# Two edits in one: expert low parts on VectorE alone with pinned one-hot rows, and bytes left unused ahead of pools so that both operands of a matmul begin at the same offset modulo 512

## The chip, the cores and the metric

The kernel runs on one core of a Trainium2 chip. A core has TensorE (PE), VectorE (DVE), ScalarE (ACT), GpSimd (POOL) and the sync engine (SP), which issues most of the DMAs. The metric is the device time of the whole program in microseconds.

## What is computed

A diffusion-style block of two layers is followed by a second block with a mixture of experts. There are 1024 tokens of width 1024. Cut to what matters here:

```python
def even_mixer(hx, ...): qa, ..., gb = split_cols(h @ w_in, ...)      # layer 0: attention, then w_out
def gla_mixer(hx, ...):  q, k, v, g, ... = h @ w_in                    # layer 1: gated linear attention, then w_out

def mixer_layer(u, ...):                                               # second block, 1040 rows (16 are meta tokens)
    a, bv, bg, q, k, v, fg, gates = split(u @ w_in)
    ya = pool_mixer(a, ...) @ w_out_a
    yb = conv_module(bv, bg, ...) @ w_out_b
    yc = forgetting_attention(heads(q), heads(k), heads(v), logf) @ w_out_c
    return (g[:, :, 0] * ya + g[:, :, 1] * yb + g[:, :, 2] * yc) @ w_o

def hier_moe(t, ...):                                                  # 16 experts, the top 2 of one group for each token
    for e in range(N_EXPERTS):
        he = silu(t @ exp_w1[e]) * (t @ exp_w3[e])
        y = y + comb[:, e:e + 1] * (he @ exp_w2[e])

return rms_norm_2(h[:, N_META:], final_g)
```

All products are of float32 inputs.

## The kernel before

**Products in three parts.** A float32 operand is split in two fp32r tiles: the high part `h` is a cast by ScalarE (L161), the low part `l` is the operand less its high part, a subtraction (L164). `split_into` does both; its last argument puts the subtraction on VectorE ("v") or GpSimd ("p"). `mm3` then adds three products in PSUM: L168, L169 and L170 are high by high, low by high and high by low. In the trace `pj<-sloth,u2h` reads: into `pj`, moving operand `sloth` (a weight slot's high part, 512 columns wide), stationary operand `u2h` (128 rows wide).

**Stages**, in order, by the time of the profile: projections of layer 0 from `h0`, up to 490 us; its attention, to 850; the Bridge (`omT` times w_out) and layer 1's projections from `h1`, to 1310; the scans of layer 1, to 1465; the second Bridge, to 1545; the projections of the mixer from `u2`, to 2091; fox (the forgetting attention), to 2240; the merge (products `my` of `yabT` and `ycT`), to 2365; w_o (again `omT`) with the router, to 2485; the experts, to 2758; the tail with the last adds and the final norm, to 2793.5.

**Experts.** Tokens are gathered into 24 tiles of 128: experts 0 to 6 have two tiles, the others one, and the two kinds alternate; a 17th group takes what overflows. For each tile, `turned` transposes the gathered rows `xg` into `xT`, `hidden` computes `ph` (24 products by `w13`) and `he`, `hidden_turned` transposes `he` to `hT`, and `result` computes `y` (12 products by `w2`), which is added to `acc` in DRAM by an indirect DMA. An expert's weights come as six raw pieces of 512 KB (four `w13`, two `w2`) through 13 buffers, and each is split into its two parts. A counter sends every third low part to GpSimd. GpSimd also issues the gathers and the scatters.

**Tail.** The last two tiles' `y` is not scattered but split once more (`xTl<-y`), and added to the eight row blocks of `acc` by products with one-hot matrices (L2255): 16 tiles of 128x128, made by VectorE at L2229 in `slots_by_token`. The adds are L2256. `scaled` does the final norm of a row block: a `Square` on ScalarE into a buffer named `y`, `rr`, and a multiplication (L2244).

**What sets the order.** A scheduler orders each engine's queue when the program is built, by its own estimates; a tile that shares bytes with an older one in another pool can be written only after the older one's last use. The rest is by semaphores as the data arrives.

Of the kernel before, what the change touches and what calls it, by code (L numbers as in the profile page):

```python
# [27 lines left out]
ORD = (0, 1, 2, 3, 8, 9, 4, 5, 6, 7)  # L28
WB = 8
# [39 lines left out]
class Ctx:  # L69
    pass  # L70

# [374 lines left out]
def layer0(k, x, ctxt):  # L446
# [188 lines left out]
    with ExitStack() as es:  # L635
        kvp = es2.enter_context(tc.tile_pool(name="kv", bufs=1))
        V = kvp.tile([128, NTC, 640], F32, name="V")
# [188 lines left out]
class Bridge:  # L826
# [26 lines left out]
    def pools(self, es, res, dst, hT, off, a_col, b_col):  # L853
        self.__dict__.update(locals())
        tc = self.k.tc
        self.px = es.enter_context(tc.tile_pool(name=f"px{self.layer}", bufs=1))
        self.es2 = ExitStack()
        self.p = self.es2.enter_context(tc.tile_pool(name=f"op{self.layer}", bufs=1))

    def gate(self, c):  # L860
        g = self.p.tile([128, D], F32, name="gate")
        self.k.nc.scalar.dma_start(g, bc_rows(self.k.dgate[self.layer, c], D))
        return g

    def turn(self, i, bank=None, place=None):
        k, nc = self.k, self.k.nc
        if place:
            mt = self.row
        else:
            mt = self.p.tile([128, D], F32, name="om")  # L870
            nc.sync.dma_start(mt, self.dm[i])
        m = []
        for b in range(2):
            pt = bank() if bank else self.ps.tile([128, 4, 128], F32, name="tp", bufs=3)
            for j in range(4):
                nc.tensor.transpose(pt[:, j, :], mt[:, (4 * b + j) * 128:(4 * b + j + 1) * 128], k.ident)
            if place:
                o, t = Ctx(), place(b)
                o.h, o.l = t[:, 0], t[:, 1]
            else:  # L880
                o = Split(self.p, [128, 4, 128], "omT", 3)
            split_into(k, pt, o.h, o.l)
            m.append(o)
        return m
# [327 lines left out]
T2 = S + NM  # L1212
LAGF = 3
# [23 lines left out]
def mixer2(k, br, x1, x2):  # L1237
# [20 lines left out]
    with es:  # L1258
        hp = es.enter_context(tc.tile_pool(name="u2", bufs=1))
        uT = Split(hp, [128, 8, T2], "u2")  # L1260
        g1 = k.vec["norm1"]
        es3 = ExitStack()
        br.pools(es3, lambda i: x1[i], lambda i: x2[i], uT, NM, g1[:, None, :], None)
# [18 lines left out]
        tslices = [(0, 348), (348, 346), (694, 346)]  # L1282
# [256 lines left out]
    yp = es0.enter_context(tc.tile_pool(name="ycT", bufs=1))  # L1539
    ycT = Split(yp, [128, 4, S], "ycT")  # L1540
    NB = NT + 1
    with ExitStack() as es:
        kvp = es.enter_context(tc.tile_pool(name="fkv", bufs=1))

        p2, p = (es.enter_context(tc.tile_pool(name=n, bufs=1)) for n in ("fw2", "fw"))
        wo = k.wo = Ctx()
# [193 lines left out]
def moe(k, dm, x2, out):  # L1740
# [53 lines left out]
    with ExitStack() as es:  # L1794
# [189 lines left out]
        def row(name):  # L1984
            return mp.tile([128, 16], F32, name="R" + name)
# [59 lines left out]
        pc2 = mp.tile([128, 1], F32, name="pc2")  # L2045
# [24 lines left out]
    def tiles(raw_tile, groups, keep=0, hooks=None, ahead=1, pre=()):  # L2070
# [5 lines left out]
        def expert_split(raws):  # L2076
            w13 = Split(p, [128, 8, 512], "w13", 1 + ahead)
            w2 = Split(p, [128, 2, 1024], "w2", 2)
            yield w13, w2
            for q in range(2):  # L2080
                for a in range(2):
                    k.ndma += 1
                    c = (slice(None), slice(4 * q, 4 * q + 4), slice(256 * a, 256 * a + 256))
                    split_into(k, next(raws), w13.h[c], w13.l[c], "a", "v" if k.ndma % 3 else "p")
                    yield
            for q in range(2):
                k.ndma += 1
                split_into(k, next(raws), w2.h[:, q, :], w2.l[:, q, :], "a", "v" if k.ndma % 3 else "p")
                yield
# [10 lines left out]
        def turned(t, x):  # L2100
# [5 lines left out]
            xT = Split(p, [128, 8, 128], "xT", 2)  # L2106
            for b in range(2):
                pt = ps.tile([128, 4, 128], F32, name="xt", bufs=4)
                for j in range(4):
                    nc.tensor.transpose(pt[:, j, :], x[:, (4 * b + j) * 128:(4 * b + j + 1) * 128], k.ident)  # L2110
                split_into(k, pt, xT.h[:, 4 * b:4 * b + 4], xT.l[:, 4 * b:4 * b + 4])
            return xT, w
# [107 lines left out]
    def slots_by_token():  # L2220

        fg.append(raw_tile([128, D]))
        nc.scalar.dma_start(fg[0], bc_rows(A["final_g_2"], D))
        for t in last_tiles:
            sm = mp.tile([128, NT], F32, name="sm", bufs=KEEP)
            nc.vector.tensor_scalar(sm, th, -1.0, sl[:, t:t + 1], op0=OP.mult, op1=OP.add)
            P = raw_tile([128, NT, 128], F32R)
            for i in range(NT):
                nc.vector.tensor_scalar(P[:, i, :], cnt, sm[:, i:i + 1], None, op0=OP.is_equal)  # L2229
            to.append(P)  # L2230

    def rows():

        for i in range(NT):
            X.append(raw_tile([128, D]))
            nc.sync.dma_start(X[i], acc[i * 128:(i + 1) * 128, :])

    def scaled(p, i):
# [3 lines left out]
        nc.scalar.activation(p.tile([128, D], F32, name="y", bufs=2), x, AF.Square, accum_out=ss)  # L2242
# [4 lines left out]
    es, p, ps, kept = tiles(raw_tile, groups, KEEP, {-KEEP - 1: slots_by_token, -KEEP: rows}, pre=[chain(pre, rest)])  # L2247
    for i in range(NT):
# [8 lines left out]
        scaled(p, i)  # L2257
# [3 lines left out]
    with tc.If(nx > NXS):  # L2261
        with tc.tile_pool(name="exraw2", bufs=1) as rp2:
# [6 lines left out]
            for i in range(NT):  # L2269
                nc.sync.dma_start(X[i], acc[i * 128:(i + 1) * 128, :])  # L2270
                scaled(rp2, i)
# [43 lines left out]
```

## Time and profile before

| | |
|---|---|
| time, median of 3 runs | 2800.44 us (2799.43 to 2801.71) |
| profiled execution | 2795.24 us, span 2793.5 us |
| granted TensorE clock, mean | 0.979 |
| TensorE busy | 2645.3 us, 95% of the span, 15970 matmuls |
| VectorE, ScalarE, GpSimd busy | 55%, 38%, 21% |
| DMA | 405.33 MB, 145 GB/s on average |

A matmul's duration is modelled and overlaps the next; where TensorE doesn't stand still, the time between two starts is what a matmul costs. Idle time is read from the waits: an engine, the line it waited in, and what released it.

### The profile page before, as it was taken

How to read it: one execution, taken by the hardware profiler on the slowest of the kernel's cores; microseconds unless marked ns; L12 is line 12 of the kernel's file. 1: busy time of each engine (PE TensorE's matmuls, PEld its weight loads, DVE VectorE, ACT ScalarE, POOL GpSimd, SP SyncE). 2: the span in 40 equal slices, each digit the busy share in tenths (PEclk: the TensorE clock that was granted, in tenths of full speed). 3: DMA queues.
4: the chain of work that ended last, by engine and by line, in shares of the span. 5: the costliest groups of instructions: out<-in, count | busy, mean ns of one | idle time of the engine just before them, and what ended most of it. 6: DMA issues, size and time to landing. Idle time of an engine off the chain costs nothing. (4 is left out here: it accounts for less than half of the span.)

```text
span 2793.5 us, 41767 instructions
## 1 busy us (share of the span) xinstructions
PE 2645.3 (95%) x15970; PEld 2172.5 (78%) x15970; DVE 1536.0 (55%) x2972; ACT 1066.6 (38%) x2035; POOL 580.9 (21%) x515
## 2 busy tenths in 40 slices
PE   8999999999999999999999999999999999969995
PEld 3777778887887778887887887788878977857774
DVE  5467747887886461100884434373206655357886
ACT  4333321666663332112642332222316621246563
POOL 1334400012211110012541120000000033025662
PEclk9999999999999999999999999999999999979998
DMA  7233387546224353222654123232437157449995
GB/s 249 83 90 106 114 214 213 183 92 121 66 51 164 108 184 106 86 76 101 200 193 151 60 84 106 91 117 83 125 122 174 32 165 253 143 171 325 312 317 173
DMA packets 273570, 405.33 MB, mean 145 GB/s; under 512 B 28338, under 2 KB 156585, under 8 KB 272721
## 3 DMA queue, kind: packets, MB, share of 16 engines
q1 hardware_dynamic: 255360, 365.79, 42.7%
q0 software_dynamic: 6624, 24.14, 3.4%
q10 hardware_dynamic: 11376, 12.64, 1.4%
q8 instruction: 128, 2.10, 0.3%
q14 instruction: 82, 0.66, 0.1%
HBM read 290.35 MB, written 112.15 MB: 144 GB/s over the span
## 5 line engine op out<-in xcount | busy, mean ns | idle before, releaser
L164 DVE TENSOR_TENSOR slotl<-slotraw,sloth 128x1024 fp32r<-128x1024 f32 (+2 forms) x100 | 116.8, 1170 | 282.7 <-ACT sloth L161 226.6
L168 PE MATMUL pj<-sloth,u2h 128*128 128x512 f32 (+1 forms) x592 | 237.4, 401 | 0.0
L169 PE MATMUL pj<-slotl,u2h 128*128 128x512 f32 (+1 forms) x592 | 234.8, 397 | 0.0
L170 PE MATMUL pj<-sloth,u2l 128*128 128x512 f32 (+1 forms) x592 | 233.2, 394 | 0.0
L168 PE MATMUL pj<-wh,h0h 128*128 128x512 f32 (+1 forms) x560 | 216.2, 386 | 0.3 <-DVE h0h L338 0.3
L169 PE MATMUL pj<-wl,h0h 128*128 128x512 f32 (+1 forms) x560 | 212.3, 379 | 0.5 <-DVE wl L164 0.4
L170 PE MATMUL pj<-wh,h0l 128*128 128x512 f32 (+1 forms) x560 | 211.4, 378 | 0.0
L169 PE MATMUL pj<-slotl,h1h 128*128 128x512 f32 x432 | 168.7, 391 | 0.0
L168 PE MATMUL pj<-sloth,h1h 128*128 128x512 f32 x432 | 168.7, 390 | 0.0
L170 PE MATMUL pj<-sloth,h1l 128*128 128x512 f32 x432 | 168.5, 390 | 0.0
L161 ACT CAST sloth<-slotraw 128x1024 fp32r<-128x1024 f32 (+2 forms) x100 | 99.6, 999 | 152.8 <-PE my L170 62.5
L168 PEld LDWEIGHTS pj<-sloth,u2h 128*128 128x128 f32 (+1 forms) x592 | 110.0, 186 | 28.3 <-issue 1.0
L170 PEld LDWEIGHTS pj<-sloth,u2l 128*128 128x128 f32 (+1 forms) x592 | 110.0, 186 | 28.3
L169 PEld LDWEIGHTS pj<-slotl,u2h 128*128 128x128 f32 (+1 forms) x592 | 110.0, 186 | 26.8 <-issue 1.0
L168 PEld LDWEIGHTS pj<-wh,h0h 128*128 128x128 f32 x560 | 106.7, 191 | 20.7 <-issue 2.0
L169 PEld LDWEIGHTS pj<-wl,h0h 128*128 128x128 f32 x560 | 107.1, 191 | 19.4 <-DVE wl L164 1.6
L170 PEld LDWEIGHTS pj<-wh,h0l 128*128 128x128 f32 x560 | 106.4, 190 | 19.6
L164 DVE TENSOR_TENSOR w13l<-raw,w13h 128x1024 fp32r<-128x1024 f32 x51 | 106.0, 2092 | 1.6 <-ACT w13h L161 1.1
L736 ACT ACTIVATE Pb<-Pb,stb 128x1280 f32<-128x1280 f32 (+1 forms) x80 | 94.9, 1188 | 29.9 <-DVE stb L735 29.6
L168 PE MATMUL pj<-sloth,omTh 128*128 128x512 f32 x256 | 103.3, 404 | 0.5 <-ACT omTh L161 0.5
L775 POOL TENSOR_TENSOR mt<-mt,gt 128x256 f32<-128x256 f32 x20 | 14.7, 737 | 422.9 <-DVE mt L771 219.6
L170 PE MATMUL pj<-sloth,omTl 128*128 128x512 f32 x256 | 101.6, 398 | 0.0
(614 smaller groups left out, 6707.9 us busy)
## 6 DMA issues: line engine op xcount, KB each, us to landing
raw<-in_exp_w_dram SPq DMA_DIRECT2D x102, 512.0 KB
Q<-dq SPq DMA_DIRECT2D x40, 512.0 KB
slotraw<-in_w_in_dram SPq DMA_DIRECT2D x40, 512.0 KB
mraw<-in_adaln_w_dram SPq DMA_DIRECT2D x64, 256.0 KB
wraw<-in_ab_w_in_dram SPq DMA_DIRECT2D x24, 512.0 KB
slotraw<-in_gla_w_in_dram SPq DMA_DIRECT2D x24, 512.0 KB
fg<-po SPq DMA_DIRECT2D x48, 256.0 KB
g<-fg SPq DMA_DIRECT2D x16, 768.0 KB
```

Source lines behind the costliest of these rows:

```text
L161: nc.scalar.copy(hi, src)
L164: (nc.vector if lo_eng == "v" else nc.gpsimd).tensor_sub(lo, src, hi.bitcast(F32))
L168: nc.tensor.matmul(out, lh, rh, start=first, stop=False)
L169: nc.tensor.matmul(out, lh, rl, start=False, stop=False)
L170: nc.tensor.matmul(out, ll, rh, start=False, stop=last)
L736: nc.scalar.activation(P[:, :nk], P[:, :nk], AF.Exp, bias=mc, scale=-1.0, accum_out=sm)
L775: nc.gpsimd.tensor_mul(ma, ma, t.gt[:, ca])
```

## The change

It joins two edits.

First, `PADS` puts unused bytes at the start of some pools, and the rows of `u2` get 1152 elements instead of 1040, so that a row is a multiple of 512 bytes. `gate` and `om` of the second Bridge go into places of `yab`, a few small tiles change their pool, and the channel part of the mixer takes its columns in slices of 272, 384 and 384. The offsets modulo 512 at which the two operands of the 512-column products begin, by the addresses in the built programs:

| products | number | moving | stationary before | stationary after |
|---|---|---|---|---|
| layer 0, `h0` | 1680 | 0 | 0 | 0 |
| layer 1, `h1` | 1296 | 480 | 480 | 480 |
| Bridges, `omT` | 816 | 480 | 288, 128 or 0 | 480 |
| mixer, `u2` | 1776 | 480 | a multiple of 64 | 480 |
| merge, `ycT` | 384 | 480 | 0 | 480 |
| w_o, `omT` | 384 | 480 | 480, and 192 for 120 of them | 480 |
| experts, `w13` and `w2` | 864 | 256, after 32 | 384 | 32 |

48 of the `u2` products had equal offsets by chance. Some products of 256 columns or fewer (attention, fox) change too.

Second, all low parts of the experts go to VectorE, the 16 one-hot rows are made by `one_hot` from hooks and kept in program order, and `Square` in `scaled` writes into an `xg` buffer instead of `y`.

```diff
--- before.py
+++ after.py
+PADS = dict(kv=480, op0=192, op1=448, u2=416, fw=256, ycT=480, xT=384)
...
+def pad(pool, n, name="pad"):
+    if n:
+        pool.tile([128, n // 4], F32, name=name)
...
         kvp = es2.enter_context(tc.tile_pool(name="kv", bufs=1))
+        pad(kvp, PADS["kv"])
...
 T2 = S + NM
+U2 = 1152
...
         hp = es.enter_context(tc.tile_pool(name="u2", bufs=1))
-        uT = Split(hp, [128, 8, T2], "u2")
+        pad(hp, PADS["u2"])
+        uT = Split(hp, [128, 8, U2], "u2")
-        br.pools(es3, lambda i: x1[i], lambda i: x2[i], uT, NM, g1[:, None, :], None)
+        br.pools(es3, lambda i: x1[i], lambda i: x2[i], uT, NM, g1[:, None, :], None, places=yab)
...
     yp = es0.enter_context(tc.tile_pool(name="ycT", bufs=1))
+    pad(yp, PADS["ycT"])
         kvp = es.enter_context(tc.tile_pool(name="fkv", bufs=1))
         p2, p = (es.enter_context(tc.tile_pool(name=n, bufs=1)) for n in ("fw2", "fw"))
+        pad(p, PADS["fw"])
         wo.ps = ps = wo.es.enter_context(tc.tile_pool(name="fps", bufs=1, space=PSUM))
...
-        tslices = [(0, 348), (348, 346), (694, 346)]
+        tslices = [(0, 272), (272, 384), (656, 384)]
...
             yield w13, w2
             for q in range(2):
                 for a in range(2):
-                    k.ndma += 1
                     c = (slice(None), slice(4 * q, 4 * q + 4), slice(256 * a, 256 * a + 256))
-                    split_into(k, next(raws), w13.h[c], w13.l[c], "a", "v" if k.ndma % 3 else "p")
+                    split_into(k, next(raws), w13.h[c], w13.l[c])
                     yield
             for q in range(2):
-                k.ndma += 1
-                split_into(k, next(raws), w2.h[:, q, :], w2.l[:, q, :], "a", "v" if k.ndma % 3 else "p")
+                split_into(k, next(raws), w2.h[:, q, :], w2.l[:, q, :])
                 yield
         last = []
...
             with behind():
                 nc.vector.tensor_mul(w, x[:, D:D + 1], fst[:, t:t + 1])
                 nc.vector.scalar_tensor_tensor(w, x[:, D + 1:D + 2], snd[:, t:t + 1], w, op0=OP.mult, op1=OP.add)
-            xT = Split(p, [128, 8, 128], "xT", 2)
+            if not xT:
+                pad(p, PADS["xT"], "pad2")
+            xs = Split(p, [128, 8, 128], "xT", 2)
             for b in range(2):
                 pt = ps.tile([128, 4, 128], F32, name="xt", bufs=4)
                 for j in range(4):
                     nc.tensor.transpose(pt[:, j, :], x[:, (4 * b + j) * 128:(4 * b + j + 1) * 128], k.ident)
-                split_into(k, pt, xT.h[:, 4 * b:4 * b + 4], xT.l[:, 4 * b:4 * b + 4])
-            return xT, w
+                split_into(k, pt, xs.h[:, 4 * b:4 * b + 4], xs.l[:, 4 * b:4 * b + 4])
+            return xs, w
         def hidden(xT, w13):
             ph = ps.tile([128, 512], F32, name="ph", bufs=2)
...
         fg.append(raw_tile([128, D]))
         nc.scalar.dma_start(fg[0], bc_rows(A["final_g_2"], D))
-        for t in last_tiles:
-            sm = mp.tile([128, NT], F32, name="sm", bufs=KEEP)
-            nc.vector.tensor_scalar(sm, th, -1.0, sl[:, t:t + 1], op0=OP.mult, op1=OP.add)
-            P = raw_tile([128, NT, 128], F32R)
-            for i in range(NT):
-                nc.vector.tensor_scalar(P[:, i, :], cnt, sm[:, i:i + 1], None, op0=OP.is_equal)
-            to.append(P)
+        to.extend(raw_tile([128, NT, 128], F32R) for _ in last_tiles)
+    def one_hot(m):
+        sm = mp.tile([128, NT], F32, name="sm", bufs=KEEP)
+        nc.vector.tensor_scalar(sm, th, -1.0, sl[:, last_tiles[m]:last_tiles[m] + 1], op0=OP.mult, op1=OP.add)
+        for i in range(NT):
+            tc.keep_in_program_order(nc.vector.tensor_scalar(to[m][:, i, :], cnt, sm[:, i:i + 1], None, op0=OP.is_equal))
     def rows():
         for i in range(NT):
             X.append(raw_tile([128, D]))
             nc.sync.dma_start(X[i], acc[i * 128:(i + 1) * 128, :])
-
-    def scaled(p, i):
+        one_hot(0)
+    def scaled(p, i, sq):
         x = X[i]
         ss = p.tile([128, 1], F32, name="ss", bufs=4)
-        nc.scalar.activation(p.tile([128, D], F32, name="y", bufs=2), x, AF.Square, accum_out=ss)
+        nc.scalar.activation(sq, x, AF.Square, accum_out=ss)
         rr = rstd_of(k, p, ss, 1, 1.0 / D, f"rr{i % 4}")
         nc.vector.scalar_tensor_tensor(x, x, rr, fg[0], op0=OP.mult, op1=OP.mult)
         nc.sync.dma_start(out[i], x)
-    es, p, ps, kept = tiles(raw_tile, groups, KEEP, {-KEEP - 1: slots_by_token, -KEEP: rows}, pre=[chain(pre, rest)])
+    es, p, ps, kept = tiles(raw_tile, groups, KEEP, {-KEEP - 1: slots_by_token, -KEEP: rows, 1 - KEEP: lambda: one_hot(1)},
+                            pre=[chain(pre, rest)])
     for i in range(NT):
         x = X[i]
         for h in range(2):
...
                 for q in range(2):
                     nc.tensor.matmul(po, to[m][:, i, :], yp[q][:, 4 * h:4 * h + 4], start=(m == q == 0), stop=(m == KEEP - 1 and q == 1))
             nc.vector.tensor_add(x[:, c], x[:, c], po)
-        scaled(p, i)
+        scaled(p, i, p.tile([128, D + 2], F32, name="xg", bufs=2)[:, :D])
     es.close()
     nx = nc.values_load(odx[0:1, NE + NX:NE + NX + 1], min_val=0, max_val=NX)
```

Line numbers move: L161 and L164 become L169 and L172, L168 to L170 become L176 to L178, L2119 becomes L2134, L2229 becomes L2246, L2256 becomes L2274.

The built programs show what stands where on an engine. First VectorE in the experts, at the place of the trace's 2543 us, before the change: `w13l` and `w2l` are low parts of weights, `he` is the product that TensorE then transposes, `ws` and `y` scale a result, `xTl` and `hTl` are low parts of transposed rows.

```order
L164 TENSOR_TENSOR w13l<-raw,w13h 128x4x256 x2
L2119 TENSOR_TENSOR he<-he,ph 128x256
L2104 TENSOR_TENSOR ws<-xg,fst 128x1
L2105 SCALAR_TENSOR_TENSOR ws<-xg,snd,ws 128x1
L2141 TENSOR_SCALAR y<-py,ws 128x512
L164 TENSOR_TENSOR w13l<-raw,w13h 128x4x256
L164 TENSOR_TENSOR w2l<-raw,w2h 128x1024
L164 TENSOR_TENSOR xTl<-xt,xTh 128x512 x2
L164 TENSOR_TENSOR hTl<-xt,hTh 128x256
```

And at the same place after it:

```order
L172 TENSOR_TENSOR w13l<-raw,w13h 128x4x256 x2
L2134 TENSOR_TENSOR he<-he,ph 128x256
L172 TENSOR_TENSOR w13l<-raw,w13h 128x4x256 x2
L2156 TENSOR_SCALAR y<-py,ws 128x512
L172 TENSOR_TENSOR w2l<-raw,w2h 128x1024 x2
L2117 TENSOR_TENSOR ws<-xg,fst 128x1
L172 TENSOR_TENSOR xTl<-xt,xTh 128x512
L2118 SCALAR_TENSOR_TENSOR ws<-xg,snd,ws 128x1
L172 TENSOR_TENSOR xTl<-xt,xTh 128x512
L172 TENSOR_TENSOR hTl<-xt,hTh 128x256
```

Between the first `hTl` and the second there were three `w13l` and one `w2l`; now there are four `w13l` and two `w2l`, with two of the `w13l` behind `he` and ahead of `y`.

Next VectorE near the end of the last experts, before the change, where L2229 makes the one-hot rows:

```order
L164 TENSOR_TENSOR w13l<-raw,w13h 128x4x256
L2229 TENSOR_SCALAR raw<-cnt,sm 128x128 x4
L2119 TENSOR_TENSOR he<-he,ph 128x256
L2229 TENSOR_SCALAR raw<-cnt,sm 128x128 x3
L2141 TENSOR_SCALAR y<-py,ws 128x512
L2229 TENSOR_SCALAR raw<-cnt,sm 128x128
L164 TENSOR_TENSOR w13l<-raw,w13h 128x4x256
L2229 TENSOR_SCALAR raw<-cnt,sm 128x128 x8
L164 TENSOR_TENSOR w2l<-raw,w2h 128x1024
```

After it, these rows stand behind the last split of `y`, ahead of the tail's adds:

```order
L172 TENSOR_TENSOR xTl<-y,xTh 128x512
L172 TENSOR_TENSOR hTl<-xt,hTh 128x256
L172 TENSOR_TENSOR xTl<-y,xTh 128x512
L2156 TENSOR_SCALAR y<-py,ws 128x512
L172 TENSOR_TENSOR xTl<-y,xTh 128x512 x2
L2246 TENSOR_SCALAR raw<-cnt,sm 128x128 x16
L2274 TENSOR_TENSOR raw<-raw,ph 128x512
L2274 TENSOR_TENSOR raw<-raw,py 128x512
```

All 16 left the experts and are now a single block between `xTl` and the first add of `ph`.

Third, SP around fox's start, before the change: `fg` are stores of gates, `Q` is tile 1's query, `Fb` and `fV` are biases and values, `sloth` and `slotl` take keys (`fk`) and queries (`fq`) of the heads.

```order
L1485 DMA Fb_17339<-dF 128x8x128
L1491 DMA fV_17338<-fv_13541 16x512
L1489 DMA fV_17338<-fv_13533 128x512
L1564 DMA Q<-fq_13525 64x8x128 x2
L1523 DMA fg_13547<-po 128x512
L1564 DMA Q<-fq_13525 64x8x128 x2
L1523 DMA fg_13548<-po 128x512
```

After it, at the end of the gates' stores:

```order
L1484 DMA sloth<-fk 128x4x256
L1536 DMA fg_13551<-po 128x512
L1484 DMA slotl<-fk 128x4x256
L1476 DMA sloth<-fq_13528 64x4x128
L1579 DMA Q<-fq_13527 64x8x128 x4
L1498 DMA Fb_17935<-dF 128x8x256
L1502 DMA fV_17934<-fv_13536 128x512
```

The four loads of `Q` moved from amid the stores of `fg` to behind the last of them, behind key and query loads and ahead of tile 1's `Fb` and `fV`. The pool `fw`, which holds `Q`, now overlaps a tile of the mixer's stage by 64 bytes.

## Rows read from the trace of the kernel before

**Rows 1.** Windows: length; busy PE, PEld, DVE, ACT, POOL; clock, DMA share, GB/s.

```profile
1180.00:1300.00 120.00, 120.00 (x531) 99.37 (x530) 5.79 (x6) 18.73 (x27) 20.00 (x18) 1.00 0.20 68
1830.00:1940.00 110.00, 110.00 (x475) 88.92 (x474) 59.09 (x48) 20.32 (x28) 0.00 (x0) 1.00 0.27 91
2520.00:2730.00 210.00, 193.85 (x938) 158.94 (x937) 176.08 (x204) 129.48 (x192) 130.65 (x68) 1.00 1.02 314
```

**Rows 2.** Timeline of TensorE in w_o: start, duration, instruction.

```profile
2405.76 0.39 PE L168 MATMUL my<-sloth,omTh 128*128 128x512 f32 x1
...
2409.84 0.39 PE L168 MATMUL my<-sloth,omTh 128*128 128x512 f32 x1
...
2432.18 0.40 PE L168 MATMUL my<-woh,omTh 128*128 128x512 f32 x1
...
2434.28 0.40 PE L168 MATMUL my<-sloth,omTh 128*128 128x512 f32 x1
...
2436.35 0.39 PE L168 MATMUL my<-sloth,omTh 128*128 128x512 f32 x1
```

**Rows 3.** Timeline of TensorE in the experts.

```profile
2540.19 0.39 PE L168 MATMUL ph<-w13h,xTh 128*128 128x512 f32 x1
...
2544.61 0.39 PE L169 MATMUL ph<-w13l,xTh 128*128 128x512 f32 x1
```

**Rows 4.** Waits from 2480 on: total us, times, longest.

```profile
PE xt L2126 <- DVE he L2119: 16.2, 8, 2.4
...
PE py L170 <- DVE hTl L164: 7.3, 1, 7.3
...
POOL acc L2067 <- DMA raw<-in_exp_w_dram: 0.7, 1, 0.7
```

**Rows 5.** Groups of low parts, 2520 to 2730, forms apart.

```profile
L164 DVE TENSOR_TENSOR w13l<-raw,w13h 128x1024 fp32r<-128x1024 f32 x43 | 96.3, 2254 | 1.3 <-ACT w13h L161 0.8
...
L164 POOL TENSOR_TENSOR w2l<-raw,w2h 128x1024 fp32r<-128x1024 f32 x14 | 39.0, 2784 | 0.1
...
L164 POOL TENSOR_TENSOR w13l<-raw,w13h 128x1024 fp32r<-128x1024 f32 x15 | 38.7, 2583 | 14.8 <-DVE ws L2105 5.9 <-ACT w13h L161 4.7 <-POOL w2l L164 4.2
...
L164 DVE TENSOR_TENSOR w2l<-raw,w2h 128x1024 fp32r<-128x1024 f32 x14 | 17.0, 1216 | 0.0
```

**Rows 6.** Timeline of all engines around one wait for `he`.

```profile
2543.30 7.62 DVE L164 TENSOR_TENSOR w13l<-raw,w13h 128x1024 fp32r<-128x1024 f32 x2
...
2546.72 3.12 POOL L164 TENSOR_TENSOR w13l<-raw,w13h 128x1024 fp32r<-128x1024 f32 x1 [0.20 <-POOL w2l L164]
...
2551.30 0.44 PE L2126 MATMUL xt<-ident,he 128*128 128x128 f32 x2 [2.41 <-DVE he L2119]
```

**Rows 7.** Timeline of VectorE and TensorE around the wait for `hTl`.

```profile
2729.82 5.10 DVE L2229 TENSOR_SCALAR raw<-cnt,sm 128x128 fp32r<-128x128 f32 x8
...
2741.13 0.80 PE L170 MATMUL py<-w2h,hTl 128*128 128x512 f32 x1 [7.27 <-DVE hTl L164]
...
2744.71 0.53 PE L169 MATMUL py<-w2l,hTh 128*128 128x512 f32 x1
```

**Rows 8.** Window behind that wait, columns as in rows 1.

```profile
2741.70:2744.70 3.00, 3.00 (x8) 2.32 (x7) 2.29 (x4) 0.00 (x0) 0.00 (x0) 0.50 0.00 0
```

**Rows 9.** Timeline of VectorE: one-hot rows, and the tail.

```profile
2727.25 0.67 DVE L2229 TENSOR_SCALAR raw<-cnt,sm 128x128 fp32r<-128x128 f32 x3
...
2770.36 0.15 DVE L297 TENSOR_SCALAR rr<-ss 128x1 f32<-128x1 f32 x1 [2.54 <-ACT y L2242]
```

**Rows 10.** Timeline of SP, TensorE and VectorE at fox's start.

```profile
1988.32 2.82 SPq L1564 DMA_DIRECT2D Q<-fq  x2
...
2094.85 0.37 SPq L1485 DMA_DIRECT2D Fb<-dF  x1
...
2099.15 0.74 PE L1593 MATMUL sc<-sloth,Q 128*128 128x256 f32 x4
...
2104.71 0.35 DVE L1607 CUSTOM_DVE_ANT_0 P<-sc,Fb,st 128x128 f32<-128x128 f32 x1 [1.96 <-DMA Fb<-dF]
```

More of the change, by code (lines that the diff above doesn't have):

```diff
@@ L851, in ahead, with pools @@
         self.es.close()
-    def pools(self, es, res, dst, hT, off, a_col, b_col):
+    def pools(self, es, res, dst, hT, off, a_col, b_col, places=None):
         self.__dict__.update(locals())
@@ L858, in pools @@
         self.p = self.es2.enter_context(tc.tile_pool(name=f"op{self.layer}", bufs=1))
+        pad(self.p, PADS[f"op{self.layer}"])
     def gate(self, c):
-        g = self.p.tile([128, D], F32, name="gate")
+        g = self.p.tile([128, D], F32, name="gate") if self.places is None else self.places[:, 0]
         self.k.nc.scalar.dma_start(g, bc_rows(self.k.dgate[self.layer, c], D))
@@ L869, in turn @@
         else:
-            mt = self.p.tile([128, D], F32, name="om")
+            mt = self.p.tile([128, D], F32, name="om") if self.places is None else self.places[:, 1]
             nc.sync.dma_start(mt, self.dm[i])
@@ L1984, in row @@
         def row(name):
-            return mp.tile([128, 16], F32, name="R" + name)
+            return (p if name in ("key", "nt", "two") else mp).tile([128, 16], F32, name="R" + name)
         def total(name, t):
@@ L2044, in moe @@
         V.tensor_scalar(em_, sl, 0.0, None, op0=OP.is_lt)
-        pc2 = mp.tile([128, 1], F32, name="pc2")
+        pc2 = p.tile([128, 1], F32, name="pc2")
         V.tensor_scalar(pc2, pc, float(S), None, op0=OP.add)
@@ L2270, in moe @@
                 nc.sync.dma_start(X[i], acc[i * 128:(i + 1) * 128, :])
-                scaled(rp2, i)
+                scaled(rp2, i, raw2([128, D]))
     es0.close()
```

## The prediction

> **What bounds the kernel now.** I first read windows of the stages, for who is busy. TensorE works 193.85 of 210 us in the experts and all of the time in the long projections [rows 1], so what counts is how often a matmul starts and where TensorE stands still. I then looked at the starts in the timeline, since a single matmul's 0.39 us overlaps its neighbours.
>
> A 512-column matmul of the h1 projection starts every 120/531 = 226.0 ns, one of u2 every 110/475 = 231.6 ns (both counts take in edge rows) [rows 1]. Both windows have the full clock and no TensorE idle time. In h1 the two operands begin at the same offset modulo 512, in u2 they do not. That could be the stage, so I looked for both kinds within one: in w_o, 18 intervals from 2405.76 to 2409.84 with offsets (480, 480) give 226.7 ns, and 9 from 2432.18 to 2434.28 with (480, 192) give 233.3. The 9 that follow, again (480, 480), give 230.0 [rows 2]. So the offset goes with a price, and equality doesn't always earn all of it. The experts (256, 384) run at 19 intervals in 4.42 us, 232.6 ns [rows 3].
>
> Then the waits from 2480 on: TensorE waits 16.2 us in 8 pieces for VectorE's `he`, and once 7.3 us for `hTl` [rows 4]. The forms of the low parts say why: between 2520 and 2730 a 128x1024 piece takes VectorE 1216 ns for `w2l` but 2254 on average for `w13l`, while GpSimd runs pieces of 2.6 to 2.8 us [rows 5]. In the timeline two `w13l` pieces take 7.62 us, from 2543.30, with a GpSimd piece of the same kind (2546.72, 3.12 us) inside; `he` is queued behind them, and TensorE resumes at 2551.30 after 2.41 us [rows 6].
>
> **Offsets.** About 3912 matmuls change from unequal to equal: u2 1728, the two Bridges 816, experts 864, merge 384, w_o 120. From h1 and u2 the price is 5.6 ns [rows 1], so at most 3912 x 5.6 = 21.9 us. The crowded equal run gains only 232.6 - 230.0 = 2.6 ns [rows 2, 3], which gives 10.2 us. Nearly all these matmuls lie in long runs like those of h1, so I take 5.2 ns: **-20.4 us**. TensorE is the bound in all of these stages, so that shortens the path. No row shows equal offsets made by padding; zero is kept as a bound, a rival below. The padding itself issues nothing. New slices of the u2 channels have the same sum of columns, so I cost them at nothing; their cover is TensorE's full window, and a slice more would cost a row load of about 0.2 us.
>
> A rule speaks against this. The Trainium skill, "SBUF — State Buffer", section "SBUF: two separate sides", says that only the port pair shared by GpSimd and VectorE contends and that TensorE never waits on anyone; "TensorE: Matmul & The Clock Gate", "Step-by-step: what each phase is for", gives the moving and the stationary operand a read port each. By these, placement in SBUF is worth 0, and the sum below becomes -19.2 us. The w_o rows disagree with that, since they differ in nothing else that I can see [rows 2]; hence a small chance.
>
> **Low parts.** 34 pieces leave GpSimd, 29 of them in that window, where VectorE spends 96.3 + 17.0 = 113.3 us on its own 57 [rows 5]. If a long piece is long because GpSimd works beside it, all 86 cost 86 x 1.22 = 104.9 us: the pieces that shrink pay for the added ones, and VectorE falls from 176 us of 210 to some 168 [rows 1]. What was late, `he`, comes after two pieces of 1.22: from 2543.30 it would start at 2545.7 instead of some 5 us later [rows 6], more than the 2.41 us waited. So **-16.2 us** [rows 4]. Next in line is `hTl`: after `he` the queue now holds four pieces (4.9 us), `y` (0.75), `ws` (0.4), two `xTl` (1.3) and `hTl` (0.4), 7.8 us, against a tile's TensorE time of 36 x 0.2326 plus some 1.3 us of transposes, 9.7 us. One to two microseconds of margin: thin, and a source of the upper end. The casts stay on ScalarE. The raw weights don't limit: the list names them for GpSimd alone, with 0.7 us at most [rows 4], though the DMA share is 1.02 [rows 1]; the stage gets 7% shorter, and if the loads can't follow, part of the 16.2 stays.
>
> The 7.3 us wait ends at 2741.13, and from there up to 2744.71 matmuls start every 3.58/8 = 448 ns; the window there has a granted clock of 0.50, the lower of TensorE's two levels (1.2 GHz) [rows 7, 8]. Against 232 that is 8 x 0.216 = 1.7 us more. Ahead of it stand eight one-hot rows that take 5.10 us from 2729.82 [rows 7]. They leave this place, and the pieces shrink: **-9.0 us**.
>
> **The tail.** The 16 one-hot rows now stand between the last `xTl` and the first add, in a stretch where VectorE sets the pace. Three take 0.67 us without GpSimd [rows 9], about 0.2 each: +3.2 us, or up to 16 x 0.64 = 10 us at the price of the eight [rows 7]. GpSimd has no low parts left there, so I take 3.2. Against it, `Square` no longer writes into `y`, which the `ykept` DMA releases late; before 2770.36 VectorE stood 2.54 us for that `Square` [rows 9]. Net **+1 us**, from 0 to +7.
>
> **Fox start.** Before, SP issues tile 1's four Q loads from 1988.32 on, a hundred microseconds ahead. After, they stand behind the last fk and fq loads and ahead of `Fb` and `fV`, because the fw pool now shares bytes with a tile of the u2 stage. SP's first issue after that wait is `Fb` at 2094.85; now Q is, and its pairs took 2.82 us to issue before (5.5 for four). `Fb`, `fV` and later fq are queued behind. TensorE first wants Q at 2099.15; VectorE already waits 1.96 us for `Fb` at 2104.71 [rows 10]. `Fb`, issued from 2094.85 on, is used 10 us later; Q issued in its place and landed as slowly comes near 2105, 6 us late; the delays of Q and `Fb` overlap. At best 1 MB hurries and 2 us are lost, at worst 12 with both in a row. I take **+5 us**.
>
> **Sum.** -20.4 - 16.2 - 9.0 + 1 + 5 = -39.6 us. The profiled execution took 2795.24 us (span 2793.5), so 2755.6; the runs' median, 2800.44, lies 5.2 us above it, hence **2761 us** for the median. The likeliest case's own range is 2750 to 2771.
>
> **Rivals.**
> 1. *Placement is worth nothing or half.* For it: the crowded equal rows. Against it: the two w_o stretches [rows 2]. Then 2781 (nothing) or 2771 (half).
> 2. *The experts keep their stalls.* `hTl` slips past its margin of 1 to 2 us, or the loads don't follow. With half of 25.2 us kept: 2774; all: 2786. Against it: GpSimd's place in the long pieces [rows 6].
> 3. *The other side: VectorE becomes the bound of the experts.* If 2254 ns is the price of a piece that follows another without a pause, the 29 added cost 65 us, and VectorE needs 176 + 65 - 4 (one-hot rows that leave) = 237 us for what takes 210. It decides once a piece averages (210 - 176.1 + 113.3 + 4)/86 = 1.76 us. Over all 24 tiles instead of the window's 20 that is 27 x 1.2 = 32 us more; the stalls and the experts' own 4.5 us of offsets bring nothing: -15.9 + 32 + 1 + 5 = +22, 2822. Against it: `w2l` has the same size and takes 1216 [rows 5], and 7.62 us for two coincides with GpSimd's work [rows 6].
> 4. *The fox start costs its worst case and the one-hot rows theirs*: 7 + 6 more, 2774. Against it: scores of tile 0 and of the next heads can fill some of the wait.
> 5. *More is gained than I see*: the fox start costs nothing, the whole 21.9 us of the offsets come, and the clock, 0.979 over the run against 1.00 in the long stages, gives back some 5 us where stalls vanish: 2749.
>
> **Chances.** Forecast 0.55; rival 1 0.14; rival 2 0.13; rival 3 0.04; rival 4 0.06; rival 5 0.08. 0.2% of this time, 5.6 us, is about what a measurement can tell from no change. Faster holds all but rival 3 and mixtures of 1, 2 and 4: 0.93, same 0.02, slower 0.05. For eight in ten I take 2746 to 2782: rivals 1, 4 and 5 and half of rival 2 are in, the whole of the kept stalls and rival 3 out.
>
> **What the profile after would show.** Offsets: the u2 window 1830 to 1940 with about 486 matmuls instead of 475, and expert starts at 227 ns. Low parts: `w13l` and `w2l` near 1.22 us each, all on VectorE, and no wait of TensorE for `he` above 0.5 us. One-hot rows: 16 in about 3.2 us just before the first add; no wait of ScalarE for `ykept`. Fox: Q loads of tile 1 issued after the last fg store, and a TensorE wait of some 5 us within 15 us after the first scores. The prediction is wrong if the u2 interval stays at 232, if `w13l` stays above 1.8 us, or if a wait for `hTl` comes back in each pair of tiles.

## The result, and the profile after

The changed kernel takes 2765.23 us (median of 4, 2755.8 to 2767.82) against 2801.07 us: 0.9874 of the time before, 95% interval 0.9861 to 0.9887, or 35.3 us less. The forecast was 2761 (2746 to 2782). A second measurement of the same program, with its own runs of the kernel before (`e0_changed` below), gave 0.9900 (0.9886 to 0.9914), 28 us less: two measurements of one program are 0.26% apart, and no run shows why. One run of `e5_third_p` below, 2952.83 us at a mean clock of 0.84 where its five others have 0.975 or 0.976, is left out of its median.

The profiled execution took 2755.8 us (span 2754.0), 39.4 us less than that of before; the forecast sum was -39.6. That agreement is partly luck: this execution is the fastest of the four by 9 us, and the stages differ from the forecast both ways. Their limits are the first or last rows of TensorE in the timeline: last `h0` product, last `u2`, first `yabT`, first `w13`, last `w2`, end of the span. Before these end or begin at 481.1, 2090.8, 2258.4, 2503.0, 2758.2 and 2793.5 us, after at 478.4, 2072.7, 2243.7, 2486.8, 2715.7 and 2754.0.

| stretch | before | after | after, second | difference | forecast |
|---|---|---|---|---|---|
| to the end of `h0` | 481.1 | 478.4 | 481.2 | -2.6 / +0.1 | 0 |
| to the end of `u2` | 1609.7 | 1594.3 | 1597.0 | -15.5 / -12.7 | -13.2 |
| fox | 167.5 | 171.1 | 172.8 | +3.5 / +5.2 | +5 |
| merge, w_o, router | 244.6 | 243.0 | 240.4 | -1.6 / -4.2 | -2.6 |
| experts | 255.2 | 228.9 | 231.4 | -26.4 / -23.9 | -29.7 |
| tail | 35.3 | 38.4 | 33.9 | +3.1 / -1.4 | +1 |

(Forecast of the second, fourth and fifth line: 816 + 1728, 384 + 120 and 864 matmuls at 5.2 ns, the experts with -16.2 and -9.0.)

First windows of the changed kernel in u2, at fox's start and in the experts: length; busy PE, PEld, DVE, ACT, POOL; clock, DMA share, GB/s.

```profile
1815.00:1925.00 110.00, 110.00 (x487) 91.09 (x486) 60.84 (x49) 20.24 (x28) 0.00 (x0) 1.00 0.29 96
2072.70:2092.00 19.30, 13.88 (x127) 11.16 (x128) 7.88 (x33) 9.19 (x26) 0.00 (x0) 0.82 1.04 265
2497.00:2707.00 210.00, 207.12 (x1012) 170.79 (x1011) 169.03 (x245) 138.16 (x203) 63.64 (x41) 1.00 1.04 326
```

In u2, 110 us now hold 487 matmuls where [rows 1] had 475: 225.9 ns instead of 231.6, near the 226.0 of h1. The timeline gives the same for the long products of every stage. These are means in ns between neighbouring starts of 512-column matmuls, with only gaps of 215 to 245 ns counted, so that waits and the lower clock are out:

| products | before | after |
|---|---|---|
| layer 1, `h1` (equal in both) | 227.0 | 227.0 |
| Bridges | 233.4 | 227.7 |
| mixer, `u2` | 232.3 | 227.3 |
| merge | 233.2 | 227.4 |
| w_o (120 of 384 unequal before) | 229.5 | 227.9 |
| experts | 232.3 | 227.8 |

In the experts TensorE is busy for 207.1 of 210 us instead of 193.9, GpSimd for 63.6 instead of 130.7, and VectorE, with all low parts, for 169 instead of 176.

The low parts in the groups of 2480 to 2690, forms apart, and TensorE's waits from 2487 to 2715:

```profile
L172 DVE TENSOR_TENSOR w13l<-raw,w13h 128x1024 fp32r<-128x1024 f32 x58 | 69.0, 1218 | 1.5 <-ACT w13h L169 1.0 <-issue 0.2 <-DMA raw<-in_exp_w_dram 0.2
L172 DVE TENSOR_TENSOR w2l<-raw,w2h 128x1024 fp32r<-128x1024 f32 x30 | 35.4, 1216 | 3.8 <-ACT w2h L169 3.8
```

```profile
PE py L178 <- DVE hTl L172: 1.6, 2, 1.0
PE xt L2125 <- DMA xg<-vd,gix: 1.3, 1, 1.3
PE py L176 <- ACT hTh L169: 1.0, 1, 1.0
```

`w13l` fell from 2254 to 1218 ns, what `w2l` took already [rows 5]; 88 pieces cost VectorE 104.4 us. The waits for `he` [rows 4] are gone, the 7.3 us for `hTl` too. A new one stands second: TensorE waits for the gathered rows `xg`, for which it did not wait between 2503 and 2758 before.

At fox's start, the timeline of SP, VectorE and TensorE in the changed kernel:

```profile
2073.70 0.33 SPq L1536 DMA_DIRECT2D fg<-po  x1
...
2073.72 0.50 PE L1608 MATMUL sc<-sloth 128*128 128x256 f32 x2 [1.03 <-ACT po L1534]
...
2076.94 2.54 SPq L1579 DMA_DIRECT2D Q<-fq  x4
2077.22 0.42 DVE L1622 CUSTOM_DVE_ANT_0 P<-sc,Fb 128x256 f32<-128x256 f32 x1 [48.41 <-DMA fg<-po]
...
2077.70 0.79 PE L1608 MATMUL sc<-sloth 128*128 128x256 f32 x2 [3.04 <-DVE st L1622]
...
2085.84 0.48 PE L1608 MATMUL sc<-sloth,Q 128*128 128x256 f32 x2
```

The delay is there, but not where I put it. The last `fg` store is issued at 2073.70; the first softmax of fox, on VectorE, waits for it until 2077.22, and TensorE for that softmax. `Q`, also held until the store lands (2076.94), is there when TensorE wants it at 2085.84: no wait. The two score matmuls at 2077.70 take 0.79 us where the two at 2073.72 took 0.50, and the window from 2072.7 to 2092 has a mean granted clock of 0.82, so part of it ran at the lower level (1.2 GHz).

The tail, TensorE's timeline:

```profile
2719.85 0.47 PE L2273 MATMUL ph<-xTh,raw 128*128 128x512 f32 x1 [4.20 <-DVE raw L2246]
```

TensorE waits 4.2 us for the one-hot rows, which VectorE makes in 3.22 us from 2719.42 on, once the last `xTl` is done: most of the wait is for VectorE to come to them, and the first product follows 0.4 us later.

### The profile page after: what moved, and what is told of

The parts are those of the page before. It is cut to its first block, busy times and chain, and to the rows that moved or that the text cites. A ratio compares the mean times of both kernels' runs of the same rounds, so it can differ in the third digit from the quotient of the medians.

```text
span 2754.0 us, 41730 instructions
## 1 busy us (share of the span) xinstructions
PE 2627.1 (95%) x15970; PEld 2174.4 (79%) x15970; DVE 1515.2 (55%) x3006; ACT 1067.5 (39%) x2035; POOL 498.7 (18%) x481
## 4 chain that ended last, share of the span: by engine, by line
PE 74%; DVE 9%; DMA 7%; POOL 4%; issue 3%; ACT 2%; SPq 1%; DVEq 0%; ACTq 0%; POOLq 0%
PE pj L176 12%; PE pj L177 12%; PE pj L178 12%; PE tp L672 3%; PE tp L763 3%; PE sc L739 2%; PE my L176 2%; PE my L178 2%; PE my L177 2%; POOL rr L555 2%; DVE qu L568 2%; PE sc L1608 2%; PE tp L719 2%; PE tp L1642 2%; PE tp L1634 1%
## 5 line engine op out<-in xcount | busy, mean ns | idle before, releaser
L172 DVE TENSOR_TENSOR slotl<-slotraw,sloth 128x1024 fp32r<-128x1024 f32 (+2 forms) x100 | 118.5, 1186 | 280.8 <-ACT sloth L169 277.7
L176 PE MATMUL pj<-sloth,u2h 128*128 128x512 f32 (+1 forms) x592 | 233.9, 395 | 0.0
L178 PE MATMUL pj<-sloth,u2l 128*128 128x512 f32 (+1 forms) x592 | 230.8, 390 | 0.0
L176 PE MATMUL pj<-wh,h0h 128*128 128x512 f32 (+1 forms) x560 | 216.6, 387 | 0.0
L178 PE MATMUL pj<-wh,h0l 128*128 128x512 f32 (+1 forms) x560 | 212.6, 380 | 0.0
L176 PE MATMUL pj<-sloth,h1h 128*128 128x512 f32 x432 | 168.8, 391 | 0.0
L178 PE MATMUL pj<-sloth,h1l 128*128 128x512 f32 x432 | 168.6, 390 | 0.0
L169 ACT CAST sloth<-slotraw 128x1024 fp32r<-128x1024 f32 (+2 forms) x100 | 99.8, 999 | 153.3 <-PE my L178 55.0
L178 PEld LDWEIGHTS pj<-sloth,u2l 128*128 128x128 f32 (+1 forms) x592 | 109.6, 185 | 24.9
L176 PEld LDWEIGHTS pj<-sloth,u2h 128*128 128x128 f32 (+1 forms) x592 | 109.7, 185 | 24.8 <-issue 1.0
L176 PEld LDWEIGHTS pj<-wh,h0h 128*128 128x128 f32 x560 | 107.3, 192 | 19.8 <-DVE macc L388 0.9
L178 PEld LDWEIGHTS pj<-wh,h0l 128*128 128x128 f32 x560 | 107.1, 191 | 19.8
L176 PE MATMUL pj<-sloth,omTh 128*128 128x512 f32 x256 | 102.0, 398 | 0.5 <-ACT omTh L169 0.5
L178 PE MATMUL pj<-sloth,omTl 128*128 128x512 f32 x256 | 100.3, 393 | 0.0
L177 PE MATMUL pj<-slotl,omTh 128*128 128x512 f32 x256 | 100.1, 391 | 0.0
L1534 ACT ACTIVATE po<-pj 128x512 f32<-128x512 f32 x48 | 28.8, 599 | 183.6 <-PE pj L178 164.3
```

The lines of the kernel that those rows point to most:

```text
L169: nc.scalar.copy(hi, src)
L172: (nc.vector if lo_eng == "v" else nc.gpsimd).tensor_sub(lo, src, hi.bitcast(F32))
L176: nc.tensor.matmul(out, lh, rh, start=first, stop=False)
L177: nc.tensor.matmul(out, lh, rl, start=False, stop=False)
L178: nc.tensor.matmul(out, ll, rh, start=False, stop=last)
```

## Experiments

Ratios are to the kernel before on the same chip. Stage lengths are measured as in the table above.

**One edit at a time.** `e1_offsets` is the kernel before with the first part of the diff, `e2_experts` with the second (low parts, one-hot rows, `Square`).

> Only the offsets change (padding, wider u2 rows, places of gate and om); the experts' low parts, the one-hot rows and Square stay as before. Theory A (equal offsets save 4 to 6 ns a matmul, and the padded pools delay fox's first softmax): the u2 interval is 227 ns instead of 232, fox begins some 5 us worse, the 16.2 us of waits for he stay; about 2801 - 20 + 4 = 2785 us. Rival B (placement is worth nothing, all of the gain is in the experts): u2 stays at 232 ns and the time is 2801 to 2806. Were the two parts to overlap, this would be nearer to the whole change, below 2775.

> Only the second edit: all low parts of the experts on VectorE, one-hot rows from hooks, Square into an xg buffer; offsets as before. Theory A: the waits for he and hTl go, TensorE's interval in the experts stays at 232 ns, the tail takes some 3 us more: about 2801 - 19 = 2782 us. Rival B: 2801 - 36 = 2765, the whole gain. Rival C (VectorE becomes the bound of the experts at the slower offsets too): above 2790.

`e1_offsets` took 2784.88 us, ratio 0.9951 (0.9935 to 0.9967); `e2_experts` 2774.28, 0.9915 (0.9897 to 0.9933). Of 2800 us that is 14 and 24, together 38, against 35 and 28 for both edits at once. So each part has its gain, as theory A had it, and rival B falls in both; whether they add up in full or overlap by some microseconds these measurements can't tell.

In `e1_offsets` all stages run at 227 to 228 ns, the stretch to the end of u2 takes 1599.1 (-10.6) and fox 171.4. The experts take 257.3, no less than before although their matmuls start 4.5 ns sooner. The waits for `he` are no longer than they were (16.3 us in 8, before 16.2). What takes the gain back is the clock: after three of these waits, of 2.1 to 2.5 us each, six or seven matmuls start every 427 ns, at the lower level, where before all eight went by without that. The 19 of them cost 3.8 us, as much as 864 x 4.4 ns. TensorE's waits there, and a window behind the third:

```profile
PE xt L2143 <- DVE he L2136: 16.3, 8, 2.5
PE py L178 <- DVE hTl L172: 8.0, 2, 7.3
```

```profile
2709.00:2711.80 2.80, 2.80 (x8) 2.18 (x7) 2.80 (x4) 1.04 (x2) 1.64 (x2) 0.50 1.09 371
```

In `e2_experts` the intervals stay as before (232 to 234 ns where the offsets differ), and the experts take 234.5, 20.8 less. Its merge, w_o and router take 242.0 us, 2.6 less than before, and its stretch to the end of u2 1612.7, 2.9 more, with their offsets unchanged: single profiles of a stage differ by that much.

**u2's offset alone.** The changed kernel with u2 moved on, everything behind it put back:

```diff
-PADS = dict(kv=480, op0=192, op1=448, u2=416, fw=256, ycT=480, xT=384)
+PADS = dict(kv=480, op0=192, op1=384, u2=480, fw=256, ycT=480, xT=384)   # e3_u2_64
+PADS = dict(kv=480, op0=192, op1=192, u2=672, fw=256, ycT=480, xT=384)   # e3_u2_256
```

> The changed kernel with u2 alone moved on by 64 bytes (offsets 480 and 32 for its 1728 products), all the other products equal as in it. Theory A: 1728 x 5 ns = 8.6 us more than the changed kernel, 2774 us, and 232 ns between starts in the u2 stage while h1 and the merge stay at 227. Rival B: the wider rows of u2, not the offset, brought its gain: no change, 2765, 227 ns.

> The changed kernel with u2 alone moved on by 256 bytes (offsets 480 and 224). Theory A (only equality modulo 512 helps): again 2774 us and 232 ns in the u2 stage. Rival B (what counts repeats every 256 bytes or less): 2765 us and 227 ns.

Windows of 110 us inside the same u2 run, first with 64 bytes (offsets 480 and 32), then with 256 (480 and 224), columns as above:

```profile
1825.00:1935.00 110.00, 110.00 (x473) 88.64 (x472) 60.81 (x49) 19.59 (x27) 0.00 (x0) 1.00 0.28 94
```

```profile
1818.00:1928.00 110.00, 110.00 (x487) 91.09 (x486) 61.13 (x49) 20.29 (x28) 0.00 (x0) 1.00 0.29 97
```

473 against 487. With 64 bytes the time is 2774.14 us, ratio 0.9912 (0.9897 to 0.9927), and the stretch to the end of u2 1606.5 us; with 256 bytes 2766.54, 0.9886 (0.9868 to 0.9903), and 1595.3. The two intervals of the ratio overlap a little, but the runs, all on one chip, do not: 2770.9 to 2776.1 against 2758.1 to 2769.1 us. The layout is otherwise the same, so theory A holds for 64 bytes: the offset itself has the price, not the wider rows. For 256 bytes rival B holds: an offset that differs by 256 costs nothing. Of what was tried, what must agree is the start modulo 256. The kernel before fits: `u2` stood an odd multiple of 32 bytes off its weights, the experts 128, the merge 480, w_o's unequal part 288, and all of them paid.

**The experts' offset alone.**

```diff
-PADS = dict(..., xT=384)
+PADS = dict(..., xT=0)
```

> The changed kernel without the padding ahead of the experts' xT: their 864 products have offsets 32 and 160, all others are equal as in it. Theory A: 864 x 4.5 ns = 3.9 us more, 2769 us, 232 ns between starts in the experts, no new waits. Rival B (in the experts VectorE's chain to hTl sets the pace, not TensorE's interval): the interval grows but the waits shrink by as much, 2765.

2761.13 us, ratio 0.9869 (0.9850 to 0.9888), not above the changed kernel. TensorE's `ph` starts every 232.4 ns again, yet the experts take 231.5 us, against 228.9 and 231.4 in the two profiles of the changed kernel and 231.9 to 232.6 in four other kernels with its experts. Rival B's result holds as far as the runs can tell, by another way: the wait that shrinks is that for `xg`, 1.6 us here, 1.3 in the first profile of the changed kernel and 2.5 to 4.8 in the other five. Of the 3.9 us, 0 to 2.6 were gained.

**GpSimd back.** A third of the low parts again with "p" in `expert_split`:

```diff
-                    split_into(k, next(raws), w13.h[c], w13.l[c])
+                    k.ndma += 1
+                    split_into(k, next(raws), w13.h[c], w13.l[c], "a", "v" if k.ndma % 3 else "p")
```

> The changed kernel with every third low part of the experts on GpSimd again. Theory A (GpSimd's pieces make VectorE's long): w13l on VectorE is 2.2 us on average again, TensorE waits some 16 us for he, 2765 + 16 to 20 = 2781 to 2785 us. Rival B (the one-hot rows amid the experts and the offsets made those waits): waits for he below 3 us and 2765 to 2768.

2778.09 us, ratio 0.9935 (0.9917 to 0.9953): 17 us above the changed kernel by its first measurement, 10 by the second. The experts take 247.6 us, 16 to 19 more. Low parts from 2500 to 2710, and TensorE's waits in the experts:

```profile
L172 DVE TENSOR_TENSOR w13l<-raw,w13h 128x1024 fp32r<-128x1024 f32 x43 | 95.5, 2235 | 1.5 <-ACT w13h L169 1.5
...
L172 POOL TENSOR_TENSOR w13l<-raw,w13h 128x1024 fp32r<-128x1024 f32 x14 | 37.0, 2644 | 10.9 <-DVE ws L2120 4.5 <-ACT w13h L169 4.3 <-POOL w2l L172 1.9
```

```profile
PE xt L2143 <- DVE he L2136: 19.4, 8, 3.2
PE py L176 <- ACT hTh L169: 0.9, 1, 0.9
```

The same `w13l` on VectorE is 2235 ns on average with GpSimd's pieces beside it and 1218 without. Theory A holds, and with it the forecast's reading of [rows 5].

The run also tells what made the wait for `hTl`. GpSimd's pieces are back, but the one-hot rows stand behind the experts, and no wait for `hTl` is left; in `e1_offsets`, with the rows in their old place, it is 7.3 us again. In `e9_hot_early` below the rows stand amid the experts without GpSimd's pieces: all 16 take 3.23 us, and `hTl` is 1.1 us late at most. As far as these three runs tell, it took the rows there at the price that they have beside GpSimd.

**Fox's overlap.** The `cn` tiles leave the pool of the u2 stage's outputs, so that `fw` no longer lies over it:

```diff
-            cn[i] = ep.tile([128, 256], F32, name="cn", bufs=2)
+            cn[i] = bp.tile([128, 256], F32, name="cn", bufs=2)
```

> The changed kernel with the two cn tiles taken from another pool, so that fox's small tiles and Q no longer lie over the pool of the u2 stage's outputs. Theory A (the first softmax of fox waits for the last store of fg because of that overlap, and Q is issued late for the same reason): Q is issued ahead again, the 3.0 us wait of TensorE after the first scores and the half clock behind it go, 3 to 5 us less, 2760 to 2762. Rival B (the wait belongs to the stage's end and only changes its name): no change, 2765.

2758.27 us, ratio 0.9855 (0.9835 to 0.9875). Fox takes 168.2 us, against 171.1 to 172.8 in the ten profiles of kernels in which `fw` lies over that pool. VectorE and TensorE in its timeline, and the window of fox's first 19 us:

```profile
2079.22 0.42 DVE L1622 CUSTOM_DVE_ANT_0 P<-sc,Fb 128x256 f32<-128x256 f32 x1 [45.73 <-PE sc L1618]
...
2079.71 0.50 PE L1608 MATMUL sc<-sloth 128*128 128x256 f32 x2 [0.36 <-DVE st L1622]
```

```profile
2077.40:2096.60 19.20, 15.33 (x143) 11.82 (x145) 9.08 (x40) 10.53 (x31) 0.00 (x0) 0.92 0.99 247
```

The loads of `Q` are issued from 1983 on again. The first softmax waits for scores, not for a store, TensorE 0.36 us instead of 3.04, and the clock is 0.92 instead of 0.82. Theory A, with a caution: without the overlap fox took 167.5 (before), 168.2 (here) and 169.6 (the last run below), but 171.4 in `e2_experts`, where TensorE waited 2.5 us for VectorE at the first `Q` scores and 1.5 us for a later load of `fq`. The stage's own spread is near the effect; the place of the wait is what shows it. Nor is all that this kernel gained in time fox's: its stretch to the end of u2, 1591.7 us, is 2.6 and 5.3 below the changed kernel's.

**Square.** `scaled` gets a `y` buffer again:

```diff
-        scaled(p, i, p.tile([128, D + 2], F32, name="xg", bufs=2)[:, :D])
+        scaled(p, i, p.tile([128, D], F32, name="y", bufs=2))
```

> The changed kernel with Square writing into the y buffer again, as before the change. Theory A: ScalarE again waits for the ykept DMA, VectorE in the tail stands 2 to 3 us more, 2767 to 2768. Rival B (in the changed kernel the one-hot rows cover that wait): no change, 2765.

2767.17 us, ratio 0.9886 (0.9869 to 0.9904): within the two measurements of the changed kernel. Its tail is 41.4 us against 38.4 and 33.9, and ScalarE waits:

```profile
2739.35 1.06 ACT L2259 ACTIVATE y<-raw 128x1024 f32<-128x1024 f32 x1 [11.82 <-DMA ykept<-y]
```

The wait is as theory A says; the 3 us that this tail is longer than the longest of the changed kernel show in the profile and not clear of the noise in the time.

**The same program again, the one-hot rows earlier, and a third gather buffer**, on one chip (the diff is cut):

```diff
         to.extend(raw_tile([128, NT, 128], F32R) for _ in last_tiles)
+        one_hot(0)                                   # e9_hot_early; not from the later hooks
+        one_hot(1)
...
-NRAW = 13                                            # e11_xg3_raw12
+NRAW = 12
-... p.tile([128, D + 2], F32, name="xg", bufs=2)
+... p.tile([128, D + 2], F32, name="xg", bufs=3)
```

> The changed kernel itself once more, beside the two that follow, to see how far two executions of the same program differ. Theory: 0.987 of the time before; the stages after layer 0's projections as in its first profile within 2 us, the first 40 us within 5 us of it.

> The changed kernel with the 16 one-hot rows made three tiles before the end, ahead of two w2l pieces, instead of behind the last xTl. Theory A (the rows delay the first add of the tail, TensorE waits 4.2 us for them there): the tail from the last py to the end gets 3 to 4 us shorter; in the experts hTl comes some 2 us late once; 2 us less in all, 2763 us. Rival B (the tail is bound by VectorE's adds and multiplications whatever stands ahead): no change, 2765.

> The changed kernel with three xg buffers instead of two, so that a gather can be issued one tile earlier; for the room, 12 raw buffers instead of 13. Theory A (the experts now wait for gathers, 1.3 to 4.8 us in the profiles so far): no wait of TensorE for xg, 3 to 4 us less, 2761 us. Rival B (the DMA engines are full, share 1.02, so earlier issues only move the wait): the wait goes to the raw weights or to hTl and the time stays, 2765, or grows by the missing raw buffer.

`e0_changed` 2767.04 us, 0.9900 (0.9886 to 0.9914); `e9_hot_early` 2761.49, 0.9872 (0.9854 to 0.9889); `e11_xg3_raw12` 2764.14, 0.9887 (0.9872 to 0.9903). With the early rows the tail takes 32.6 us, the least so far, and the experts 233.1: theory A in direction. With three buffers no wait for `xg` is left from the second tile on, and the experts take 228.5 us against 231.4, as theory A says; the tail, 37.7, gives it back in that profile, where TensorE waits 5.3 us for the one-hot rows, and the time is not clear of the noise. The missing raw buffer shows in no wait of TensorE.

**All three.** `cn`, early rows, three `xg` buffers with 12 raw ones.

> The changed kernel with the three edits together: cn in the other pool, three xg buffers with 12 raw ones, and the one-hot rows three tiles before the end. Theory (each removes a wait of another stage, so they add up): fox 168 us instead of 171 to 173, the experts 228 to 230, the tail 33 to 34; 8 to 10 us below the changed kernel, a ratio to the kernel before near 0.984. Rival (they share the wait for full DMA engines in the experts, so the earlier one-hot rows cost there what they save in the tail): 4 to 5 us below the changed kernel, by cn alone, 0.986.

2754.61 us (2746.62 to 2756.47), ratio 0.9850 (0.9824 to 0.9875): the fastest median, but `e6_cn` alone has 0.9855 (0.9835 to 0.9875), so the rival is as good as the theory. Fox takes 169.6, the tail 31.5 and the experts 231.9 us. TensorE's waits say what the experts paid, and so does the window behind the longest:

```profile
PE py L178 <- DVE hTl L172: 4.1, 4, 2.4
```

```profile
2707.20:2710.00 2.80, 2.80 (x7) 2.22 (x8) 2.80 (x4) 0.00 (x0) 0.80 (x1) 0.50 0.15 41
```

`hTl` is 2.4 us late at 2707.1, right behind the one-hot rows (2699.8 to 2703.0), and the clock is at the lower level behind it; the margin of one to two microseconds is used up there. No wait for `xg` is left in the experts.

## Why the prediction held, step by step

- **Offsets, -20.4.** Right in mechanism and in the price of a matmul: the intervals of the table times the numbers of products give 20.0 us (and 3912 x 5.2 is 20.3), and moving u2 by 64 bytes takes its part back. In the length of a stage it shows for u2 and the Bridges (-12.7 and -15.5 for -13.2). For the merge and w_o (-1.6 and -4.2 for -2.6) it doesn't, since `e2_experts` is as far off without it; there only the interval shows it. The experts' part of 4.5 us was mis-sized: 0 to 2.6 in the changed kernel, none in `e1_offsets`. There the lower clock took it back; in the changed kernel the waits for gathers may, but no run has unequal offsets and three gather buffers.
- **The "crowded" 230.0 ns** of [rows 2] was misread. These intervals follow straight on an unequal run: the seven from 2434.28 to 2435.90 average 231 ns, the next four 226.5. In the changed kernel, where all offsets agree, w_o has the same: seven intervals from 2400.54 to 2402.16 average 231 ns, then 25 average 226.4. A run needs some matmuls to settle, so equal offsets do earn it all in long runs.
- **The rule against it.** The Trainium skill says in "SBUF — State Buffer", section "SBUF: two separate sides", that TensorE never waits on anyone. The forecast read this as a placement worth nothing; 473 against 487 matmuls in one window speak against that reading.
- **Low parts, -16.2.** Right: the waits for `he` are gone, and 19.4 us return with GpSimd, with 16 to 19 us in the length of the experts. Rival 3, VectorE as the bound, falls with `w13l` at 1218 ns. The thin margin for `hTl` is real: 1.2 to 1.6 us of waits for it remain.
- **hTl and the half clock, -9.0.** Right: the 7.3 us wait is gone with the one-hot rows, and from `e1_offsets` to `e5_third_p`, which differ in the rows and `Square`, the experts fall from 257.3 to 247.6 us, 9.7 less, with what the lower clock cost behind the waits. All told the experts gave 23.9 to 26.4 for 29.7: the rest is of the size of the experts' offsets, the waits for `xg`, and 2 to 3 us for `hTh` and `hTl`.
- **Tail, +1.** -1.4 and +3.1 in two executions of one program; the sign is open. The one-hot rows cost 3.2 us as forecast, and TensorE waits for them.
- **Fox, +5.** 3.5 and 5.2, but the step was wrong in how. I had `Q` and `Fb` land late; neither holds TensorE. The first softmax waits for the last `fg` store, because fox's tiles lie over the pool of the u2 stage's outputs, and the clock falls behind that wait. TensorE's wait there is 3.0 us, not some 5. That the size of the stage came out is luck.
- **The rest.** -2.6 us of the profiled difference lie ahead of `h0`'s end, in code that did not change. The changed kernel's seven other runs lie 6 to 13 us above the profiled one of their measurement (2755.8 and 2758.5), with mean clocks of 0.973 to 0.978 against 0.979; why, no run settles. It is 5 us for the kernel before, and I carried that over: here the median is 9.4 us above the profiled execution, and that is all of the 4 us between 2761 and 2765.

## What to carry to other kernels

Where TensorE is the bound, compare the time between starts across stages, not a matmul's duration: two stages of one shape with different intervals point at where the operands lie, a stage that holds both kinds gives the price before any run, and moving one tile settles it. Moving work off a helper engine can pay for itself on the engine that takes it, when the helper's pieces were what made that engine's own pieces long. And padding moves every pool behind it: look in the built order for loads that lost their early place, and ask of every tile that now shares bytes, not only of the load, who waits for the old owner.

## What the runs showed of the hardware

- Back to back, 512-column fp32r matmuls start every 226.9 to 228.4 ns (means of a stage, over all 14 profiles) when their operands' offsets agree modulo 256, and every 232.3 to 233.5 when not, for differences of 128, 192, 448 and 480 bytes and odd multiples of 32 alike. Agreement modulo 512 isn't needed: 256 apart gave 227.3 ns in the u2 stage, 64 apart 233.3.
- A 128x1024 subtraction on VectorE takes 1218 ns alone and 2235 to 2254 on average beside GpSimd's. One-hot rows of 128x128 take 0.20 us each without GpSimd's pieces (16 in 3.23) and 0.64 beside them (eight in 5.10).
- After waits of TensorE of 2.1 to 2.5 us in the experts of `e1_offsets`, six or seven matmuls start every 427 ns, and the granted clock is 0.50 there; after others of the same length it stays at 1.00.
- The first 100 matmuls of the program, the same in all kernels, were through between 37.7 and 43.1 us in the 14 profiles, and at 37.7 and 40.7 in the two of the changed kernel.
